# Tile 4 of the band heads turned through VectorE and DRAM, in two tours of two tiles per head, and the keys' second copy on VectorE

## The chip, the cores and the metric

The kernel runs on one core of a Trainium2 chip. A core has TensorE (PE in the profile) for matrix products, VectorE (DVE), ScalarE (ACT) and GpSimd (POOL) for elementwise work, and SyncE (SP), which here issues every DMA. The metric is the device time of one execution in microseconds: a median of three runs, with the lowest and the highest beside it.

## The reference

One layer of a streaming encoder, for a prompt of 1024 rows and a sample of 32 rows with the same weights (model width 1024). After a norm, one projection gives queries, keys, values and gates for two groups of eight heads of width 64. Group A is a band attention with a softmax and a relative-position bias; group B is a stick-breaking attention, strictly causal.

```
def band_attention(q, k, v, q_pos, k_pos, bias_table):      # group A
    s = jnp.einsum('bqhd,bkhd->bhqk', q, k).astype(jnp.float32) * ATTN_SCALE
    s = s + bias_table[:, rel].astype(jnp.float32)[None]
    s = jnp.where(ok[None, None], s, NEG_INF)               # own chunk of 64 and the 8 before it
    w = jax.nn.softmax(s, axis=-1).astype(v.dtype)
    return jnp.einsum('bhqk,bkhd->bqhd', w, v)

def stick_breaking(q, k, v, q_pos, k_pos):                  # group B
    z = jnp.einsum('bqhd,bkhd->bhqk', q, k).astype(jnp.float32) * ATTN_SCALE
    log_1m = jnp.where(causal, jax.nn.log_sigmoid(-z), 0.0)
    after = lax.cumsum(log_1m, axis=3, reverse=True) - log_1m
    w = jnp.where(causal, jnp.exp(jax.nn.log_sigmoid(z) + after), 0.0).astype(v.dtype)
    return jnp.einsum('bhqk,bkhd->bqhd', w, v)

y = jnp.concatenate([oa * silu(ga), ob * silu(gb)], axis=-1) @ w_out
h = h + rmsnorm(y, g_post)
h = h + sigmoid(h @ w_ple_gate) * (p @ w_ple)
```

Everything is fp32. The keys and values of both groups are outputs too.

## The kernel before

**Numbers in two parts.** An fp32 operand is held as a high part that TensorE takes in its faster fp32r format and a low part, the rest. A product is two or three fp32r products. In the names, `kd` is the high part of a head's keys, in both halves of the 128 partitions, `kl` the low part, `L` the queries (high part in one half, low in the other), `v2` the values, `wTh` and `wTl` the turned attention weights, high and low.

**Stages.** The program records all its operations in Python and then puts them in an order (`Recorder.order`, lines 485 to 559). There is a stage "first" (norm, turning of x, first projections), eight stages 0 to 7, and a stage "last" (output projection, norm, gate). Stages 0, 2, 4 and 6 hold the attention of two A heads each (pairs A0 to A3), stages 1, 3, 5 and 7 that of two B heads each. Woven between them stand the projections of the next pair (`mm_kB`, `mm_qB`, `mm_vB` and so on), which are what TensorE does while an attention tile waits for other engines. Stages 2, 3, 6 and 7 also hold the sample's attention.

**One A head** (`attention`, line 965). The 1024 queries are eight tiles of 128. Tile i reads `cost(i)` blocks of 128 keys: 1, 2, 3, 4 for the tiles 0 to 3, and 5 (640 keys) for the tiles 4 to 7. `scores` (line 997) does the products `SA<-kdA,LA` and `SA<-kl,LA`, VectorE adds the bias and takes the minimum, ScalarE does the exponentials into `be`. Then the weights have to be turned so that keys lie on the partitions. `weights_t` (line 1060) has two ways:

- With TensorE: per block a product `ptw<-ident,be` of 128x128 into PSUM; ScalarE rounds it into `wTh`, VectorE subtracts into `wTl`.
- Through DRAM, for the tiles in `TURNED`: VectorE turns 32x32 squares (`om<-be`), and when the last tile of a tour (`ROUNDS`) is there, SyncE writes the tour to DRAM (`swapA<-om`) and reads it back with four DMAs (`wTl<-swapA`), one for each 32 partitions. Then ScalarE rounds each tile (`wTh<-wTl`) and GpSimd subtracts (`wTl<-wTl,wTh`).

Before, the A tiles 5, 6 and 7 went through DRAM, in one tour of three tiles, and the tiles 4, 0, 1, 2, 3 through TensorE. When a set of four tiles is turned, `values` (line 1106) does `PVA<-wTh,v2A` and `PVA<-wTl,v2A`; set 1 of an A head is the tiles 4 to 7, set 0 the tiles 0 to 3. B heads have three tours of one tile each, and nothing of that changes.

**The keys.** `prep_k` (line 783) makes `kd` and `kl` of a head: a copy into the head's own half of the partitions and one into the other half, both by ScalarE, and the subtraction by GpSimd. `first_head` (line 799) does the same for the very first head in two pieces.

**The order.** `Recorder.order` plays the program with rough costs. On each engine the ready operation with the smallest key goes first; the key is the place in the recorded program plus a number of `AHEAD_OF`, by engine, kind of tile and stage. Every engine then runs its list strictly in that order, and SyncE issues all DMAs in one list; before it issues a DMA it also waits for the one eight places earlier to have ended (the `DMAHW` waits in its list).

All compute instructions are issued at line 572, so the profile is read by names of tiles.

Of the kernel before, what the change touches and what calls it, by code (L numbers as in the profile page):

```python
# [15 lines left out]
SEQ = 1024  # L16
# [10 lines left out]
NT = 9  # L27
STAGES = ("first", 0, 1, 2, 3, 4, 5, 6, 7, "last")
AHEAD_OF = {
    ("ACT", "Kh"): (0, 0, 0, 0, 430, 0, 0, 0, 200, 0),  # L30
    ("ACT", "L"): (0, 0, 46, 25, 452, 0, 112, 50, 0, 0),
    ("ACT", "Qfs"): (0, 0, 0, 0, 400, 0, 0, 0, 0, 0),
# [10 lines left out]
    ("ACT", "php"): (0, 0, 0, 0, 0, 0, 0, 0, 0, 175),  # L43
    ("ACT", "ple"): (0, 0, 0, 0, 0, 0, 0, 0, 0, 315),
    ("ACT", "stk"): (0, 0, 0, 0, 0, 96, -610, 0, 0, 0),
    ("ACT", "stq"): (0, 0, 0, 0, 0, -93, 0, 0, 0, 0),
    ("ACT", "stv"): (0, 0, -42, 0, 400, 0, 0, 0, 0, 0),
    ("ACT", "v"): (0, 0, 0, 0, 461, 0, 0, 0, 0, 0),
    ("ACT", "wTh"): (0, 93, 3, 89, 487, 0, 142, 52, -161, 0),
    ("ACT", "wh"): (0, 0, 405, 0, 0, 90, -480, -51, 364, 0),  # L50
    ("ACT", "whS"): (0, 0, 0, 0, 0, 0, 0, 0, 0, -93),
    ("ACT", "whs"): (0, 0, 0, 149, 0, 0, 0, 0, 0, 0),
    ("ACT", "x"): (0, 0, 0, 0, 0, 0, 0, 0, 0, -418),
    ("ACT", "xS"): (0, 0, 0, 0, 0, 0, 0, 0, 0, 25),
    ("DVE", "Kcs"): (0, 0, 0, 530, 0, 0, 0, 0, 100, 0),
    ("DVE", "Kl"): (0, 0, 0, 0, 0, 0, 0, 421, 0, 0),
    ("DVE", "L"): (0, 0, 0, 400, 0, 0, 0, 46, 0, 0),
    ("DVE", "Qls"): (0, 0, 0, 0, 0, 0, 0, 0, 54, 0),
# [3 lines left out]
    ("DVE", "diags"): (0, 0, 0, 400, 0, 0, 0, 0, 0, 0),  # L62
    ("DVE", "hnl"): (-100, 0, 0, 0, 0, 0, 0, 0, 0, 0),
# [4 lines left out]
    ("DVE", "sum"): (0, 0, 0, -109, 0, 0, 0, 0, 0, 0),  # L68
    ("DVE", "uu"): (0, 0, 0, 0, 0, 0, 0, 0, 0, -381),
    ("DVE", "vt"): (0, 165, 0, 0, -170, -75, 367, -88, 0, 0),  # L70
    ("DVE", "wTl"): (0, 0, 70, 0, 75, 50, 0, 100, -213, 0),
# [13 lines left out]
    ("POOL", "sgg"): (0, 0, 0, 0, 0, 0, 0, 0, 200, 0),  # L85
    ("POOL", "ug"): (0, 0, 0, 0, 0, 0, 0, 0, 0, -44),
    ("POOL", "wTl"): (0, 0, 0, 0, 400, 0, 465, 0, 0, 0),
# [15 lines left out]
}  # L103

TURNED = {"A": (5, 6, 7), "B": (4, 5, 6)}
ROUNDS = {"A": ((5, 6, 7),), "B": ((4,), (5,), (6,))}
GATES = ("A0", "A1", "A2", "A3", "B0", "B1", "B2", "B3")
SHARE = {7: 8}  # L110
SETS = {"A": ((0, 1, 2, 3), (4, 5, 6, 7)), "B": ((0, 1, 2, 3), (4, 5), (6, 7))}
TILES = {"A": (5, 6, 7, 4, 0, 1, 2, 3), "B": (6, 7, 5, 4, 0, 1, 2, 3)}
LAST = (7, 6, 5, 4, 3, 2, 1, 0)
LAG_G = 1
LAG_T = 2
# [10 lines left out]
def f(ap):  # L126

    return ap.bitcast(F32)
# [449 lines left out]
def stream_step(  # L578
# [7 lines left out]
    nc = rec  # L586
# [30 lines left out]
    hnl = [hnp.tile([P, KD, CH], F32R, tag=f"hnl{c}", name=f"hnl{c}") for c in range(NCH)]  # L617
# [15 lines left out]
    qsS = const.tile([P, 4, NS], F32, tag="qsS", name="qsS")  # L633
# [137 lines left out]
    KDh, KLD, Lq, V2 = {}, {}, {}, {}  # L771

    def halves(h):
        return slice(h * HD, (h + 1) * HD), slice((1 - h) * HD, (2 - h) * HD)

    def low_keys(h):

        if h not in KLD:
            KLD[h] = opnd[h].tile([P, SEQ], F32R, tag=f"kl{h}", name=f"kl{h}")
            nc.gpsimd.memset(f(KLD[h][halves(h)[1]]), 0.0)  # L780
        return KLD[h]

    def prep_k(nm, h, st):
        r, o = halves(h)
        kd = opnd[h].tile([P, SEQ], F32R, tag=f"kd{h}", name=f"kd{nm}{h}")
        kl = low_keys(h)
        nc.scalar.copy(kd[r], st[r, 0:SEQ])
        nc.scalar.copy(kd[o], st[r, 0:SEQ])
        nc.gpsimd.tensor_tensor(kl[r], st[r, 0:SEQ], f(kd[r]), ALU.subtract)
        KDh[h] = kd  # L790

# [7 lines left out]
    def first_head(k, st, cols):  # L799

        r, o = halves(0)
        if k == "q":
            if not cols.start:
                Lq[0] = opnd[0].tile([P, SEQ], F32R, tag="L0", name="LA00")
            nc.scalar.copy(Lq[0][r, cols], st[r, cols])
            nc.vector.tensor_tensor(Lq[0][o, cols], st[r, cols], f(Lq[0][r, cols]), ALU.subtract)
            return
        if not cols.start:
            KDh[0] = opnd[0].tile([P, SEQ], F32R, tag="kd0", name="kdA00")
            low_keys(0)  # L810
        nc.scalar.copy(KDh[0][r, cols], st[r, cols])
        nc.scalar.copy(KDh[0][o, cols], st[r, cols])
        nc.gpsimd.tensor_tensor(KLD[0][r, cols], st[r, cols], f(KDh[0][r, cols]), ALU.subtract)

    def prep_v(nm, h, tok):
# [149 lines left out]
    def attention(ab, p, h):  # L965
# [31 lines left out]
        def scores(i):  # L997
# [27 lines left out]
            else:  # L1025
# [7 lines left out]
                nc.scalar.activation(w1[:, 0:n], w0[:, 0:n], AF.Exp, bias=m[:, last:last + 1], scale=-1.0, accum_out=one[:, 8 * h + i:8 * h + i + 1])  # L1033
                if h and i == TILES["A"][-1]:
                    nc.vector.reciprocal(one, one)
# [24 lines left out]
        def weights_t(i):  # L1060
# [5 lines left out]
            hi, lo = (spot(g, x, i) for x in wT[g])  # L1066
            if i in TURNED[ab]:
                tour = next(x for x in ROUNDS[ab] if i in x)
                own, _, _, group, _ = laid(g)
# [329 lines left out]
    for n in range(-1, 8):  # L1399
        a = len(order)  # L1400
        if n < 7:
            ab, p = pairs[n + 1]
# [158 lines left out]
    ple = Ple(True)  # L1561
# [75 lines left out]
    L, R = HALF  # L1637
# [17 lines left out]
    ple = Ple(False)  # L1655
# [422 lines left out]
```

## Time and profile before

| | before |
|---|---|
| median of 3 runs (lowest to highest) | 774.18 us (773.89 to 775.28) |
| the profiled execution: time, and its span | 773.29 us, 771.5 us |
| granted TensorE clock, mean | 0.999 |
| instructions in the trace | 14229 |
| DMA moved, mean rate | 165.35 MB, 214 GB/s |

The profiled execution's time is 1.79 us more than its span (what lies around the span), and 0.89 us less than the median of the runs. The prediction shows the lines of the views as it comes to them. "Busy" is the time in which an engine had an instruction under way; a wait row names the engine that waited, for what, the sum in us, how often, and the longest.

### The profile page before, as it was taken

The numbers are of one execution on the slowest core, as the hardware profiler recorded it, in microseconds if no ns is written. First come the engines' busy times: TensorE is split into PE (matmuls) and PEld (weight loads), VectorE is DVE, ScalarE is ACT, GpSimd is POOL, SyncE is SP. The second block draws the span as 40 slices with busy tenths as digits, with TensorE's granted clock in tenths as the row PEclk, the third lists the DMA queues.
The fourth block names the chain that finished last, engine by engine and source line by source line (L and its number), as shares of the span: only waits on it lengthen the run. The fifth ranks groups of instructions, "written<-read, shape, count | busy, mean of one in ns | idle before, by whom it ended". The sixth has DMA issues, their size and how long they took to land.

```text
span 771.5 us, 14229 instructions
## 1 busy us (share of the span) xinstructions
PE 757.7 (98%) x4502; PEld 703.8 (91%) x4502; DVE 577.2 (75%) x1029; ACT 543.3 (70%) x1139; POOL 507.3 (66%) x547
## 2 busy tenths in 40 slices
PE   8999999999999999899999999999999999999997
PEld 6999999999999999899999899999998877888786
DVE  6727567687688778768797578789455787898975
ACT  6557887788688768798896687555338878766461
POOL 5734778985638657569994737778552639797533
PEclk9999999999999999999999999999999999999999
DMA  8637977759776557975759888869679867759644
GB/s 294 234 116 198 251 197 228 213 145 280 160 186 191 135 153 237 248 194 172 208 173 251 191 226 203 252 179 268 174 252 309 287 206 230 261 182 384 222 146 137
DMA packets 198398, 165.35 MB, mean 214 GB/s; under 512 B 65890, under 2 KB 165386, under 8 KB 198323
## 3 DMA queue, kind: packets, MB, share of 16 engines
q1 hardware_dynamic: 198322, 164.44, 73.4%
q8 instruction: 36, 0.59, 0.3%
q14 instruction: 40, 0.32, 0.2%
HBM read 105.72 MB, written 58.91 MB: 213 GB/s over the span
## 4 chain that ended last, share of the span: by engine, by line
PE 86%; DMA 5%; SPq 3%; ACT 2%; DVE 2%; issue 1%; POOL 1%; DVEq 0%; POOLq 0%; ACTq 0%
PE mm_qA L572 6%; PE mm_kA L572 6%; PE mm_vA L572 6%; PE mm_gB L572 6%; PE mm_kB L572 6%; PE mm_vB L572 4%; PE PVB L572 4%; PE SB L572 4%; SPq L572 3%; PE mm_qB L572 3%; PE SA L572 3%; PE mm_gA L572 3%; PE PVA L572 3%; PE ple L572 3%; PE g1P L572 3%; PE o3P L572 3%
## 5 line engine op out<-in xcount | busy, mean ns | idle before, releaser
L572 POOL TENSOR_TENSOR be<-be,om 128x1024 f32<-128x1024 f32 (+8 forms) x66 | 81.5, 1242 | 47.0 <-DVE om L572 20.7
L572 DVE TENSOR_TENSOR_SCAN om<-om,SB 128x384 f32<-128x384 f32 (+5 forms) x96 | 91.5, 964 | 17.9 <-ACT om L572 10.6
L572 POOL TENSOR_TENSOR wTl<-wTl,wTh 128x640 fp32r<-128x640 f32 (+2 forms) x42 | 72.7, 1749 | 15.3 <-ACT wTh L572 9.5
L572 ACT ACTIVATE be<-SB 128x512 f32<-128x512 f32 (+5 forms) x96 | 45.7, 496 | 11.9 <-PE SB L572 8.2
L572 ACT ACTIVATE om<-SB 128x384 f32<-128x384 f32 (+5 forms) x96 | 44.4, 494 | 13.6 <-DVE SB L572 8.4
L572 ACT ACTIVATE be<-be,statA 128x640 f32<-128x640 f32 (+3 forms) x64 | 44.4, 695 | 9.4 <-DVE statA L572 9.2
L572 DVE STREAM_TRANSPOSE om<-be 128x640 f32<-128x640 f32 (+2 forms) x48 | 42.9, 899 | 2.4 <-POOL be L572 1.1
L572 ACT CAST wTh<-wTl 128x640 fp32r<-128x640 f32 (+2 forms) x48 | 35.9, 778 | 10.5 <-DMA wTl<-swapA 7.1
L572 POOL TENSOR_TENSOR oB<-oB,oB 128x256 f32<-128x256 f32 x32 | 26.5, 848 | 14.6 <-DMA oB<-in_w_out_dram 14.6
L572 POOL TENSOR_TENSOR kl<-stkB,kdB 64x1024 fp32r<-64x1024 f32 x8 | 19.7, 2461 | 20.4 <-ACT kdB L572 20.3
L572 DVE CUSTOM_DVE_ANT_0 be<-SA,biasA 128x320 f32<-128x320 f32 (+3 forms) x64 | 30.1, 480 | 3.6 <-PE SA L572 2.8
L572 PE MATMUL SB<-kl,LB 128*128 128x384 f32 (+5 forms) x96 | 32.5, 345 | 0.0
L572 PE MATMUL SB<-kdB,LB 128*128 128x384 f32 (+5 forms) x96 | 32.4, 342 | 0.0
L572 ACT CAST wTh<-ptwB 128x512 fp32r<-128x512 f32 (+3 forms) x48 | 22.8, 481 | 11.8 <-PE ptwB L572 10.1
L572 DVE TENSOR_TENSOR wTl<-ptwB,wTh 128x512 fp32r<-128x512 f32 (+3 forms) x48 | 25.9, 546 | 6.0 <-ACT wTh L572 5.2
L572 PE MATMUL SA<-kl,LA 128*128 128x320 f32 (+2 forms) x96 | 30.1, 316 | 0.0
L572 PE MATMUL SA<-kdA,LA 128*128 128x320 f32 (+2 forms) x96 | 29.9, 313 | 0.0
L572 DVE TENSOR_TENSOR SB<-SB,maskb 128x128 f32<-128x128 f32 x64 | 18.0, 293 | 15.5 <-PE SB L572 14.4
L572 DVE TENSOR_TENSOR wTl<-ptwA,wTh 128x512 fp32r<-128x512 f32 (+3 forms) x48 | 22.5, 480 | 8.1 <-ACT wTh L572 5.3
L572 POOL TENSOR_TENSOR gB<-gB,gB 128x256 f32<-128x256 f32 x32 | 24.0, 771 | 1.5 <-DMA gB<-in_w_ple_gate_dram 1.4
L572 PE MATMUL PVB<-wTl,v2B 128*128 128x256 f32 (+1 forms) x144 | 24.8, 294 | 0.0
L572 POOL TENSOR_TENSOR h<-h,x 128x512 f32<-128x512 f32 (+1 forms) x18 | 23.8, 1345 | 0.2 <-DVE h L572 0.2
(700 smaller groups left out, 2669.3 us busy)
## 6 DMA issues: line engine op xcount, KB each, us to landing
swapA<-om SPq DMA_DIRECT2D x8, 960.0 KB, 6.9
wTl<-swapA SPq DMA_DIRECT2D x32, 240.0 KB, 5.1
oB<-in_w_out_dram SPq DMA_DIRECT2D x16, 256.0 KB, 3.5
sum_dro<-oB SPq DMA_DIRECT2D x16, 256.0 KB, 3.6
gB<-in_w_ple_gate_dram SPq DMA_DIRECT2D x16, 256.0 KB, 4.4
sum_drg<-gB SPq DMA_DIRECT2D x16, 256.0 KB, 2.7
x<-in_x_prompt_dram SPq DMA_DIRECT2D x16, 256.0 KB, 3.9
h_dr<-h SPq DMA_DIRECT2D x8, 512.0 KB, 3.6
```

What stands on the lines that cost most here:

```text
L572: getattr(getattr(tc.nc, o.what[0]), o.what[1])(*args, **kw)
```

## The change

The tile sets and the order of tiles of group A:

```
-TURNED = {"A": (5, 6, 7), "B": (4, 5, 6)}
-ROUNDS = {"A": ((5, 6, 7),), "B": ((4,), (5,), (6,))}
+TURNED = {"A": (4, 5, 6, 7), "B": (4, 5, 6)}
+ROUNDS = {"A": ((4, 5), (6, 7)), "B": ((4,), (5,), (6,))}
-TILES = {"A": (5, 6, 7, 4, 0, 1, 2, 3), "B": (6, 7, 5, 4, 0, 1, 2, 3)}
+TILES = {"A": (4, 5, 6, 7, 0, 1, 2, 3), "B": (6, 7, 5, 4, 0, 1, 2, 3)}
```

The keys' second copy, in `prep_k` and in `first_head`:

```
         nc.scalar.copy(kd[r], st[r, 0:SEQ])
-        nc.scalar.copy(kd[o], st[r, 0:SEQ])
+        nc.vector.tensor_copy(kd[o], st[r, 0:SEQ])
...
         nc.scalar.copy(KDh[0][r, cols], st[r, cols])
-        nc.scalar.copy(KDh[0][o, cols], st[r, cols])
+        nc.vector.tensor_copy(KDh[0][o, cols], st[r, cols])
```

And the numbers of `AHEAD_OF`, nearly all of them, for instance:

```
-    ("SP", "swap"): (0, 415, -50, 0, 0, 0, 0, 0, 0, 0),
+    ("SP", "swap"): (0, 0, 0, 0, 0, 0, 0, 0, -200, 0),
```

What the new numbers do is seen in the order of the instructions. Three places follow.

**TensorE, stage 4, head A20** (the first head of pair A2; `A20_4` is its tile 4). Before, behind the scores of its tiles, the tile's transposes stand between products of the projection `mm_qB2` and scores of the next head A21:

```order
L572 MATMUL ptwB11_3_0_4108<-ident_160,be_193 128x128 x4
L572 MATMUL mm_qB2_1_4049<-hnh1_155,wh_qB2_0_3774 128x352
L572 MATMUL ptwA20_4_0_4117<-ident_160,be_193 128x128 x4
L572 MATMUL mm_qB2_1_4049<-hnh1_155,wh_qB2_0_3774 128x352 x2
L572 MATMUL mm_qB2_1_4049<-hnh1_155,wh_qB2_1_3785 128x352 x4
L572 MATMUL SA21_5_0_4142<-kdA21_3865,LA21_3869 128x320
L572 MATMUL PVB11_0_4135<-wTh_655,v2B11_3230 128x512
```

Now, at the same place of TensorE's list, behind the scores of head A20's last tile:

```order
L568 MATMUL SA20_3_0_4118<-kdA20_3279,LA20_3284 128x512
L568 MATMUL SA20_3_0_4118<-kl0_664,LA20_3284 128x512
L568 MATMUL SA21_4_0_4126<-kdA21_3858,LA21_3863 128x320
L568 MATMUL SA21_4_0_4126<-kl1_709,LA21_3863 128x320
L568 MATMUL mm_qB2_1_4025<-hnh1_163,wh_qB2_0_3752 128x352
L568 MATMUL mm_qB2_1_4025<-hnh1_163,wh_qB2_1_3761 128x352
L568 MATMUL PVB11_0_4097<-wTh_733,v2B11_3196 128x512
L568 MATMUL PVB11_0_4097<-wTh_733,v2B11_3196 128x384
L568 MATMUL PVB11_0_4097<-wTh_733,v2B11_3196 128x256
L568 MATMUL PVB11_0_4097<-wTh_733,v2B11_3196 128x128
L568 MATMUL ptwA20_0_0_4114<-ident_168,be_201 128x128
```

The `ptwA20_4` products are gone (a row of four and, some rows later, one of one), and the next head begins with its tile 4 instead of its tile 5.

**SyncE's list of DMAs, the same head.** Before, from the write of its one tour to the four reads (`out_4_dram<-ktB2` are outputs of keys, `gB` and `sum_drg` loads and stores of weight sums for the last stage, `o_dr` an attention result):

```order
L572 DMA swapA20_7_133<-om_179 128x1920
L572 DMA wr_qA3_0_4066<-in_w_in_dram 128x4x128
L572 DMA out_4_dram<-ktB2_3935 32x32x32
L572 DMA out_3_dram<-vtA2_3509 128x4x128
L572 DMA out_4_dram<-ktB2_3935 32x32x32 x3
L572 DMA ks_drB_91<-ktB2_3935 128x32
L572 DMA wr_qA3_1_4122<-in_w_in_dram 128x4x128
L572 DMA o_dr5_68<-otB11_1_0_3772 64x256
L572 DMA sum_drg_86<-gB220_3960 128x512
L572 DMA biasA30_4152<-r_dr_87 128x640
L572 DMA sum_drg_86<-gB120_3959 128x512
L572 DMA wTl_170<-swapA20_7_133 32x12x160 x4
```

Now, from some rows behind the first tour's write (`swapA20_5`) to the last read of the second:

```order
L568 DMA wr_qA3_1_4088<-in_w_in_dram 128x4x128
L568 DMA sum_drg_86<-gB120_3956 128x512
L568 DMA swapA20_7_138<-om_187 128x1280
L568 DMA sum_drg_86<-gB110_3958 128x512
L568 DMA biasA30_4167<-r_dr_87 128x640
L568 DMA wTl_178<-swapA20_5_137 32x8x160 x4
L568 DMA o_dr5_68<-otB11_0_0_3790 64x256
L568 DMA o_dr5_68<-otB11_0_1_3989 64x256
L568 DMA gB210_4222<-in_w_ple_gate_dram 128x512
L568 DMA wTl_178<-swapA20_7_138 32x8x160 x4
```

Where one write and four reads stood there are now two writes and eight reads, each of two tiles; the second tour's reads stand behind those of the first, and the key outputs that stood between write and reads have moved ahead of the second tour's write.

**ScalarE and VectorE, stage 3, the keys of head A20.** Before, both copies stand on ScalarE, with operations of the B head before (`SB10`) between them:

```order
L572 CAST kdA20_3295<-stkA2_3044 64x1024
L572 ACTIVATE om_179<-SB10_1_0_3253 128x256
L572 ACTIVATE be_193<-SB10_1_0_3253 128x256
L572 ACTIVATE om_179<-SB10_2_0_3254 128x384
L572 CAST kdA20_3295<-stkA2_3044 64x1024
```

Now one stands on ScalarE in that place, and the other on VectorE, between the sample's keys (`Kl0sB0`, and a transpose of the cached ones) and the low weights of head B10:

```order
L568 TENSOR_TENSOR Kl0sB0_3034<-be_201,Kh0sB0_3014 128x512
L568 CAST kdA20_3279<-stkA2_2936 64x1024
L568 STREAM_TRANSPOSE be_201<-be_201 128x512
L568 TENSOR_TENSOR wTl_178<-ptwB10_0_0_3193,wTh_733 128x128
```

Counted over the whole program, TensorE's list has 4462 products instead of 4502 (40 of `ptwA` fewer), SyncE's 40 DMAs more.

More of the change, by code (lines that the diff above doesn't have):

```diff
@@ L29 @@
 AHEAD_OF = {
-    ("ACT", "Kh"): (0, 0, 0, 0, 430, 0, 0, 0, 200, 0),
-    ("ACT", "L"): (0, 0, 46, 25, 452, 0, 112, 50, 0, 0),
-    ("ACT", "Qfs"): (0, 0, 0, 0, 400, 0, 0, 0, 0, 0),
[10 rows of a table removed]
[L43 to L57, printed above, removed]
@@ L58 @@
-    ("DVE", "Qls"): (0, 0, 0, 0, 0, 0, 0, 0, 54, 0),
[3 rows of a table removed]
-    ("DVE", "diags"): (0, 0, 0, 400, 0, 0, 0, 0, 0, 0),
-    ("DVE", "hnl"): (-100, 0, 0, 0, 0, 0, 0, 0, 0, 0),
[4 rows of a table removed]
[L68 to L71, printed above, removed]
[13 rows of a table removed]
-    ("POOL", "sgg"): (0, 0, 0, 0, 0, 0, 0, 0, 200, 0),
-    ("POOL", "ug"): (0, 0, 0, 0, 0, 0, 0, 0, 0, -44),
@@ L87 @@
-    ("POOL", "wTl"): (0, 0, 0, 0, 400, 0, 465, 0, 0, 0),
[15 rows of a table removed]
-}
-TURNED = {"A": (5, 6, 7), "B": (4, 5, 6)}
-ROUNDS = {"A": ((5, 6, 7),), "B": ((4,), (5,), (6,))}
+    ("ACT", ""): (0, 0, 0, 0, 0, 0, 0, 0, 0, 19),
+    ("ACT", "Kh"): (0, 0, 0, -265, 0, 0, 0, 0, -225, 0),
+    ("ACT", "L"): (0, 0, 0, 0, 401, 0, 200, 0, 0, 0),
+    ("ACT", "Qfs"): (0, 0, 0, 0, 398, 0, 0, 0, 0, 0),
[4 rows of a table added]
+    ("ACT", "junk"): (0, 0, 0, 0, 0, 0, 0, 0, 0, 401),
[5 rows of a table added]
+    ("ACT", "stk"): (0, 0, 0, 0, -25, 0, -120, 0, 0, 0),
+    ("ACT", "stq"): (0, 0, 0, 0, 0, 0, 167, -580, 0, 0),
@@ new lines @@
+    ("ACT", "stv"): (0, -140, 93, 0, 436, -102, 0, 0, 0, 0),
+    ("ACT", "wTh"): (0, 0, 0, 50, 400, 0, 298, 77, 0, 0),
[4 rows of a table added]
+    ("DVE", "Kcs"): (0, 0, 0, 0, 0, 0, 0, 88, 0, 0),
[4 rows of a table added]
+    ("DVE", "diags"): (0, 0, 0, 121, 0, 0, 0, 0, 0, 0),
+    ("DVE", "hnl"): (-495, 0, 0, 0, 0, 0, 0, 0, 0, 0),
[7 rows of a table added]
+    ("DVE", "wTl"): (0, -408, 441, 70, 124, 89, -87, 453, 94, 0),
[8 rows of a table added]
+    ("POOL", "Qfs"): (0, 0, 0, 0, 0, 0, 0, 0, -41, 0),
+    ("POOL", "be"): (0, 0, 203, 0, 0, 0, 359, 0, -200, 0),
+    ("POOL", "kl"): (0, 0, 0, 0, -550, 0, 0, 0, 0, 0),
@@ L109 @@
+    ("POOL", "ogg"): (0, 0, 0, 0, 0, 0, 0, 0, 86, 0),
+    ("POOL", "om"): (0, 0, 0, 0, 0, 0, -356, 0, -28, 0),
+    ("POOL", "qsS"): (0, 0, 0, 0, 0, 200, 0, 0, 0, 0),
[18 rows of a table added]
+}
+TURNED = {"A": (4, 5, 6, 7), "B": (4, 5, 6)}
+ROUNDS = {"A": ((4, 5), (6, 7)), "B": ((4,), (5,), (6,))}
 GATES = ("A0", "A1", "A2", "A3", "B0", "B1", "B2", "B3")
```

89 rows, old and new, of the table AHEAD_OF are left out of this document.

## The prediction

> **What bounds the kernel now.** First the page's busy times. TensorE (PE) is busy for nearly the whole span:
>
> ```profile
> span 771.5 us, 14229 instructions
> PE 757.7 (98%) x4502; PEld 703.8 (91%) x4502; DVE 577.2 (75%) x1029; ACT 543.3 (70%) x1139; POOL 507.3 (66%) x547
> ```
>
> Busy does not yet mean paced by itself, so next the chain of work that ended last. It shows long runs of products at one pace, and at one place something else:
>
> ```profile
> 59.91 3.80 PE mm_vA L572 x24
> 72.63 0.55 PE ptwA L572 x5
> 318.34 7.57 DMA wTl<-swapA
> 325.94 1.99 ACT wTh L572 x3
> 327.97 1.79 PE PVA L572 x10
> ```
>
> 24 products of 352 columns take 3.80 us, 0.16 us each, with nothing between: there TensorE's own work sets the time. The three rows from 318.34 on are the exception: a read of a tour, then its roundings, then the product that waited. What TensorE waits for, summed:
>
> ```profile
> PE PVA L572 <- ACT wTh L572: 2.3, 2, 2.0
> PE ptwA L572 <- DVE wlsA L572: 1.8, 2, 0.9
> PE idle L572 <- DVE newh L572: 1.3, 1, 1.3
> PE ptx L572 <- DVE be L572: 1.3, 1, 1.3
> PE PVsB L572 <- DVE Vl2sB L572: 0.8, 1, 0.8
> PE PVA L572 <- DVE v2A L572: 0.6, 1, 0.6
> PE ptwB L572 <- POOL be L572: 0.3, 1, 0.3
> ```
>
> `idle` and `ptx` are the start. The attention holds 2.3 + 1.8 + 0.8 + 0.6 + 0.3 = 5.8 us of waits, and these plus products are all that a change of the attention can gain. By stage (us, then busy us of each engine, clock, DMA share, GB/s), for A0, A2, A3 and the last B pair:
>
> ```profile
> 62.00:118.00 56.00, 56.00 (x360) 54.88 (x359) 39.18 (x90) 44.70 (x95) 35.91 (x44) 1.00 0.80 219
> 288.00:348.00 60.00, 57.96 (x381) 56.35 (x380) 46.70 (x104) 50.88 (x106) 39.78 (x37) 1.00 0.81 220
> 400.00:470.00 70.00, 68.20 (x442) 66.32 (x441) 50.12 (x109) 51.41 (x112) 40.58 (x43) 1.00 0.86 219
> 470.00:582.00 112.00, 110.88 (x718) 109.08 (x717) 80.95 (x130) 58.61 (x132) 77.90 (x84) 1.00 0.76 219
> ```
>
> TensorE idles 2.0 us in A2 and 1.8 us in A3, the A stages with the waits for `wTh`; no other engine is busy for more than 85% of an A stage, but the DMA engines are at 0.80 to 0.86.
>
> **The change part by part.** *TensorE.* Tile 4 has five blocks, so five transposes go in each of eight heads: 40. The row of five above takes 0.55 us, 0.11 us each: 40 x 0.109 = **4.4 us** less. They stand in a row of products without gaps, so all of it is on the path. Nothing is added on TensorE.
>
> *ScalarE and VectorE around the tile.* The rows, busy us in all and mean ns of one:
>
> ```profile
> L572 ACT CAST wTh<-ptwA 128x512 fp32r<-128x512 f32 x16 | 9.3, 579 | 2.0 <-PE ptwA L572 1.9
> L572 ACT CAST wTh<-ptwA 128x128 fp32r<-128x128 f32 x16 | 4.1, 275 | 1.2 <-PE ptwA L572 1.0
> L572 ACT CAST wTh<-wTl 128x640 fp32r<-128x640 f32 x32 | 21.7, 724 | 9.6 <-DMA wTl<-swapA 7.1 <-DMA be<-in_cache_a_v_dram 2.3
> L572 DVE TENSOR_TENSOR wTl<-ptwA,wTh 128x512 fp32r<-128x512 f32 x16 | 10.9, 684 | 2.5 <-ACT wTh L572 1.9 <-PE PVA L572 0.6
> L572 DVE TENSOR_TENSOR wTl<-ptwA,wTh 128x128 fp32r<-128x128 f32 x16 | 4.1, 284 | 4.3 <-ACT wTh L572 2.2 <-ACT om L572 2.0
> L572 DVE STREAM_TRANSPOSE om<-be 128x640 f32<-128x640 f32 x32 | 26.4, 832 | 1.1 <-ACT be L572 1.0
> L572 POOL TENSOR_TENSOR wTl<-wTl,wTh 128x640 fp32r<-128x640 f32 x30 | 48.7, 1645 | 9.5 <-ACT wTh L572 7.6 <-DMA oggA<-o_dr 1.6
> ```
>
> ScalarE trades 8 x (0.58 + 0.28) for 8 x 0.72, VectorE 8 x (0.68 + 0.28) for 8 x 0.83: about 1 us less on each. GpSimd takes over 8 x 1.65 = 13.2 us, 3.3 us per A stage, where it is busy for 36 of 56 us; a stage has room, so I cost it at nothing, and without that cover it is at most the 13.2.
>
> *The keys' copy.* Sixteen heads, 1.05 us each on ScalarE (half of the 14 + 16 below; the first head's two pieces taken as one more):
>
> ```profile
> L572 ACT CAST kdA<-stkA 64x1024 fp32r<-64x1024 f32 x14 | 14.7, 1048 | 4.5 <-PE SB L572 4.3
> L572 ACT CAST kdB<-stkB 64x1024 fp32r<-64x1024 f32 x16 | 16.8, 1051 | 0.3
> L572 DVE CAST wTl<-grow 1x1024 fp32r<-1x1024 f32 x1 | 0.7, 682 | 0.1
> L572 DVE CAST Vh0sB<-be 128x512 fp32r<-128x512 f32 x2 | 0.8, 405 | 0.0
> L572 DVE CAST Vh0sA<-be 128x512 fp32r<-128x512 f32 x2 | 2.5, 1232 | 3.1 <-DMA be<-in_cache_a_v_dram 3.1
> ```
>
> ScalarE loses 16.8 us. VectorE has no such copy of 64x1024 before; the nearest is 0.68 us for 1024 columns, and the bounds are those 0.68 and, from the two 512-column rows, 0.83 us more (1.23 against 0.41). I take 0.68: 11 us more on VectorE, in stages where it is busy for 75%. TensorE needs the copy only for a head's first scores, far ahead of which both queues place it: nothing on the path, 13 us (16 x 0.83) at the other end. ScalarE's gain is nothing on the path either, since no wait row of TensorE names a late copy; it may shorten the waits that end at `wTh`.
>
> The 405 and 1232 ns are one operation of one shape; here the Trainium skill has a rule that speaks against the edit: "SBUF — State Buffer", Who interferes with whom, says that a copy or cast on VectorE can take a port pair that it shares with GpSimd, and that whichever of the two starts second is blocked until the other ends. The trace agrees in that the cast's time varies threefold; that the port did it, no row shows. By the rule a copy beside the GpSimd subtraction of the same keys could stand still for all of it; what the sum would be by it is worked out from rows at the last rival below.
>
> *The tours.* 16 writes of 640 KB in place of 8 of 960, and 64 reads of 160 KB in place of 32 of 240 (each with its median us to landing, and below SyncE's time to issue):
>
> ```profile
> swapA<-om SPq DMA_DIRECT2D x8, 960.0 KB, 6.9
> wTl<-swapA SPq DMA_DIRECT2D x32, 240.0 KB, 5.1
> swapB<-om SPq DMA_DIRECT2D x8, 448.0 KB, 2.8
> wTl<-swapB SPq DMA_DIRECT2D x32, 112.0 KB, 2.9
> L572 SPq DMA_DIRECT2D wTl<-swapA x32: 563/616/736, 80.1 to 458.1; - x32
> ```
>
> Between the two sizes by bytes (37.5% of the way), a 640 KB write is 2.8 + 1.5 = 4.3 us, a 160 KB read 3.7: a round trip of 8.0 us, not 12.0. And behind the last landing stand two roundings and two subtractions instead of three (0.72 and 1.65 us less). Against it: the tour that ends last now waits for the fourth tile, not the third, and its reads stand in SyncE's list behind the four of the first tour, 4 x 0.62 = 2.5 us. So the last weights of set 1 come between 4 us earlier and, if every DMA keeps the large one's time, some 3 us later (2.5 and a tile's 0.83 turning). In the order the products that fill the time between tile 7's scores and `PVA` are about as many as before. I take **0** for the waits, with both ends kept: -2.9 us (both `PVA` rows go) and, at 3 us in the two heads that wait now, +6.
>
> *DMA.* 8 x 2 x 0.32 = 5.1 MB more: at the 219 GB/s of an A stage 5.8 us of transfers per A stage, beside the products. *The order anew* has no row: the waits for `wlsA`, `PVsB` and `ptwB` (2.9 us) can go or others come; 0.
>
> **Sum:** 773.29 - 4.4 + 0 = 768.9 for the profiled execution; the median is 0.9 above that, so **769.8 us**. A measurement of this kernel can tell about 0.2%, 1.5 us, from no change.
>
> **The rivals.** *The waits go too.* Shorter round trips and a freer ScalarE take the 2.9 us of `PVA` waits as well: 766.9, and 764.0 if all 5.8 went. For it: the largest wait stands behind three roundings in a row. Against it: it came from DMAs that landed late.
>
> *Given back at `PVA`.* The second tour begins a tile later. If `PVA` then waits 0.55 us more in each head, the 4.4 are gone; two more waits like the 2.0 of the list make 773.8. For it: two `PVA` rows already wait. Against: the smaller tours.
>
> *The DMA engines become the bound, and it is slower.* In A3, five stretches of 5 us:
>
> ```profile
> 415.00:420.00 5.00, 5.00 (x35) 4.98 (x34) 3.39 (x10) 3.39 (x11) 0.61 (x3) 1.00 1.00 312
> 420.00:425.00 5.00, 5.00 (x36) 5.00 (x35) 2.75 (x7) 3.25 (x5) 2.49 (x2) 1.00 1.16 200
> 425.00:430.00 5.00, 5.00 (x34) 4.97 (x33) 1.99 (x4) 2.62 (x7) 4.29 (x6) 1.00 1.12 247
> 430.00:435.00 5.00, 4.40 (x27) 4.01 (x26) 3.53 (x3) 3.60 (x7) 4.57 (x5) 1.00 0.89 177
> 435.00:440.00 5.00, 4.07 (x28) 3.70 (x27) 2.25 (x5) 2.08 (x5) 4.27 (x6) 1.00 0.67 154
> ```
>
> The DMA share is 1 or more for 15 us, and right behind it TensorE idles 1.5 us. If a transfer added there delays TensorE by its whole time, A2 and A3 lose 5.8 us each: 769.8 + 11.6 = 781.4. It ends slower once added waits pass 4.4 + 1.5 = 5.9 us, half of that price. Against it: A0 has a share of 0.80 and no wait at all.
>
> *The copies are held by GpSimd.* At the upper bound of 0.83 us in each of 16 heads it is 13 us of VectorE, and with half of that reaching a head's first scores 6.6: 776.4. Against it: those scores wait nowhere now. (This is where the Trainium skill's rule of "SBUF — State Buffer", Who interferes with whom, would lead.)
>
> **How the numbers follow.** Forecast 0.48 (its own range 768.0 to 771.6, from waits that come or go by 1.8 us); the waits go too 0.20; given back 0.16; DMA bound 0.11; copies held 0.05. Faster is the first two, 0.68; same 0.16; slower 0.16. The range runs from 765.5, most of the second case, to 776.0, which takes in the waits' upper end (769.8 + 6) and leaves out most of the last two.
>
> **What would show it.** Right: `ptwA` x80 and PE busy near 753; `PVA` waits of 3 us or less in all; kd casts on VectorE near 0.7 us; shorter landings of `swapA` and `wTl`. Wrong: a `PVA` wait in several heads (given back); TensorE idle behind stretches with a DMA share over 1 (DMA bound); kd casts of 1.5 us or more and waits of `SA` or `SB` products (copies held). The forecast falls if new waits anywhere, the first stage included, exceed 2 us.

## The result, and the profile after

| | time (lowest to highest) | ratio to before, 95% interval |
|---|---|---|
| before, 4 runs beside it | 774.03 us (772.6 to 775.28) | |
| changed, 4 runs | 783.74 us (781.56 to 785.63) | 1.0125 [1.0092, 1.0159] |
| the prediction | 769.8 us (765.5 to 776.0) | 0.994 |

The change costs 9.7 us; the prediction had it gain 4.4. The profiled execution took 781.56 us, span 779.8. The page of the changed kernel, busy times and the tours' DMAs:

```profile
span 779.8 us, 14229 instructions
PE 757.0 (97%) x4462; PEld 698.9 (90%) x4462; DVE 592.3 (76%) x1038; ACT 525.2 (67%) x1114; POOL 529.9 (68%) x555
swapA<-om SPq DMA_DIRECT2D x16, 640.0 KB, 3.9
wTl<-swapA SPq DMA_DIRECT2D x64, 160.0 KB, 4.3
```

TensorE has its 40 products fewer, ScalarE is 18 us less busy, the smaller tours do land sooner each (6.9 and 5.1 before). All that the change was to remove is removed. But TensorE's busy time fell by 0.7 us only (757.7 before), and the span is 8.3 us longer: TensorE idles 22.8 us in place of 13.8. Its list of waits in the changed kernel (sum in us, how often, longest):

```profile
PE PVA L568 <- ACT wTh L568: 4.1, 3, 2.3
PE PVB L568 <- ACT wTh L568: 3.9, 3, 1.6
PE PVB L568 <- DVE v2B L568: 2.9, 1, 2.9
PE ptwsA L568 <- POOL be L568: 1.3, 2, 1.0
PE ptwA L568 <- DVE wTl L568: 0.9, 1, 0.9
```

The waits before were 5.8 us in the attention; here the five rows alone are 13.1. Two kinds are new or larger: products of weights and values that wait for a rounding `wTh`, in A stages and now in B stages too, and one single wait of 2.9 us for `v2B`, which no row of before has. The three `PVB` waits for a rounding stand in stage 7, the last B pair, where no tour of group A runs; the longest of them, and the two longest of `PVA` (in A1 and A2):

```profile
505.05 0.93 PE L568 MATMUL PVB<-wTh,v2B 128*128 128x256 f32 x6 [1.62 <-ACT wTh L568]
207.64 1.50 PE L568 MATMUL PVA<-wTh,v2A 128*128 128x512 f32 x8 [1.37 <-ACT wTh L568]
334.46 1.50 PE L568 MATMUL PVA<-wTh,v2A 128*128 128x512 f32 x8 [2.31 <-ACT wTh L568]
```

Two places were followed back.

**The wait for `v2B`.** Stage 1, the values of head B00; VectorE's rows (start, us), then GpSimd's, of the changed kernel:

```profile
136.37 1.80 DVE L568 CAST kdA<-stkA 64x1024 fp32r<-64x1024 f32 x1
138.20 4.61 DVE L568 TENSOR_TENSOR v2B<-vtB,v2B 128x512 fp32r<-128x512 f32 x1
...
135.14 2.41 POOL L568 TENSOR_TENSOR kl<-stkA,kdA 64x1024 fp32r<-64x1024 f32 x1
...
137.59 1.17 POOL L568 TENSOR_TENSOR oB<-oB,oB 128x256 f32<-128x256 f32 x1
138.72 1.82 POOL L568 TENSOR_TENSOR wTl<-wTl,wTh 128x768 fp32r<-128x768 f32 x1
140.50 1.76 POOL L568 TENSOR_TENSOR be<-be,om 128x896 f32<-128x896 f32 x1
```

The new copy begins while GpSimd subtracts the low part of the same keys (`kl`, until 137.55) and ends 0.62 us behind that: 1.80 us for an operation that takes 0.69 alone. The subtraction `v2B` behind it then begins among three GpSimd operations without a gap, and ends at 142.81, 0.55 us behind the last of them (142.26): 4.61 us for one whose median is 0.93.

**A wait for `wTh`.** Stage 4, head A20, SyncE's reads of the two tours and ScalarE's roundings, of the changed kernel; then the same product `PVA` in the kernel before:

```profile
320.75 2.57 SPq L568 DMA_DIRECT2D wTl<-swapA  x4
326.11 2.98 SPq L568 DMA_DIRECT2D wTl<-swapA  x4
329.32 1.36 ACT L568 CAST wTh<-wTl 128x640 fp32r<-128x640 f32 x2 [4.67 <-DMA wTl<-swapA]
333.06 1.34 ACT L568 CAST wTh<-wTl 128x640 fp32r<-128x640 f32 x2
...
327.97 1.50 PE L572 MATMUL PVA<-wTh,v2A 128*128 128x512 f32 x8 [2.04 <-ACT wTh L572]
```

The first tour's reads are all issued by 323.32, but its rounding begins at 329.32, six microseconds later, and ScalarE stands 4.67 us at the head of its list for them. What is queued behind is late by that: 2.6 us of other work and then the second tour's rounding, for which `PVA` waits. But the second tour is late too: its last read, issued at 328.54, landed 4.3 us later, only some 0.2 us before its rounding begins. And the wait is not new: the kernel before waited 2.04 us at the same product. The 1.8 us that `PVA` waits more in all are mostly 0.42 us in A0 and the 1.37 us in A1, which it did not have.

So there were three theories. **W:** the new numbers of the order brought the waits. **D:** the turning's 5.1 MB and 40 DMAs land the weights late. **K:** a copy on VectorE is held beside GpSimd and holds what is behind it.

### The profile page after: what moved, and what is told of

Its sections match the earlier page's. It is cut to its first block, busy times and chain, and to the rows that moved or that the text cites. A ratio compares the mean times of both kernels' runs of the same rounds, so it can differ in the third digit from the quotient of the medians.

```text
span 779.8 us, 14229 instructions
## 1 busy us (share of the span) xinstructions
PE 757.0 (97%) x4462; PEld 698.9 (90%) x4462; DVE 592.3 (76%) x1038; ACT 525.2 (67%) x1114; POOL 529.9 (68%) x555
## 2 busy tenths in 40 slices
DMA packets 204156, 170.58 MB, mean 219 GB/s; under 512 B 66529, under 2 KB 170121, under 8 KB 204082
## 4 chain that ended last, share of the span: by engine, by line
PE 59%; DMA 8%; SPq 4%; ACT 4%; DVE 3%; issue 2%; POOL 1%; ACTq 0%; POOLq 0%; DVEq 0%
PE mm_gB L568 5%; PE mm_vA L568 4%; DMA wTl<-swapA 4%; SPq L568 4%; PE PVB L568 4%; PE mm_qA L568 4%; PE mm_kB L568 3%; PE o3P L568 3%; PE g1P L568 3%; PE o1P L568 3%; PE o2P L568 2%; PE o0P L568 2%; PE g0P L568 2%; PE g2P L568 2%; PE g3P L568 2%; PE SB L568 2%
## 5 line engine op out<-in xcount | busy, mean ns | idle before, releaser
L568 POOL TENSOR_TENSOR be<-be,om 128x1024 f32<-128x1024 f32 (+8 forms) x66 | 85.5, 1301 | 25.2 <-DVE om L568 18.5
L568 POOL TENSOR_TENSOR wTl<-wTl,wTh 128x640 fp32r<-128x640 f32 (+2 forms) x50 | 85.7, 1731 | 21.7 <-ACT wTh L568 10.1
L568 ACT CAST wTh<-wTl 128x640 fp32r<-128x640 f32 (+2 forms) x56 | 41.8, 773 | 30.4 <-DMA wTl<-swapA 13.1
L568 ACT ACTIVATE om<-SB 128x384 f32<-128x384 f32 (+5 forms) x96 | 44.8, 493 | 20.5 <-DVE SB L568 14.6
L568 ACT ACTIVATE be<-be,statA 128x640 f32<-128x640 f32 (+2 forms) x64 | 44.3, 693 | 13.8 <-DVE statA L568 13.6
L568 DVE STREAM_TRANSPOSE om<-be 128x640 f32<-128x640 f32 (+2 forms) x56 | 49.5, 890 | 2.3 <-POOL be L568 1.1
L568 ACT ACTIVATE be<-SB 128x384 f32<-128x384 f32 (+5 forms) x96 | 45.0, 496 | 9.2 <-PE SB L568 5.2
L568 DVE CUSTOM_DVE_ANT_0 be<-SA,biasA 128x320 f32<-128x320 f32 (+2 forms) x64 | 30.0, 480 | 4.2 <-POOL biasA L568 2.1
L568 POOL TENSOR_TENSOR oB<-oB,oB 128x256 f32<-128x256 f32 x32 | 25.8, 826 | 10.2 <-DMA oB<-in_w_out_dram 10.1
L568 PE MATMUL PVB<-wTh,v2B 128*128 128x256 f32 (+1 forms) x144 | 22.2, 286 | 6.8 <-ACT wTh L568 3.9
L568 PEld LDWEIGHTS PVB<-wTh,v2B 128*128 128x128 f32 x144 | 20.7, 188 | 8.2 <-ACT wTh L568 4.7
```

The source lines that it names most:

```text
L568: getattr(getattr(tc.nc, o.what[0]), o.what[1])(*args, **kw)
```

## The experiments

### Single edits, ordered anew

Eight kernels combine the three parts of the change: the turning, the copies, and the numbers of the order (old, new or none).

```
-TURNED = {"A": (5, 6, 7), "B": (4, 5, 6)}
+TURNED = {"A": (4, 5, 6, 7), "B": (4, 5, 6)}
...
-        nc.scalar.copy(kd[o], st[r, 0:SEQ])
+        nc.vector.tensor_copy(kd[o], st[r, 0:SEQ])
...
-    ("SP", "swap"): (0, 415, -50, 0, 0, 0, 0, 0, 0, 0),
+    ("SP", "swap"): (0, 0, 0, 0, 0, 0, 0, 0, -200, 0),
```

Turning alone: 

> The kernel before with tile 4 turned through DRAM in two tours per head; copies on ScalarE and the old numbers of the order. Theory W (the new order brings the waits): the 4.4 us of transposes are gained, so about 770 us, with a few us of misfit of the old numbers: 768 to 774. Theory D (the turning itself, its tours, 40 more DMAs and 5.1 MB, lands the weights late): 780 or more, with waits for wTh behind the DMA of swapA or swapB of 5 us more than before. Theory K (the copies on VectorE, held by GpSimd): about 770.

Copies alone: 

> The kernel before with only the keys' second copy on VectorE, old numbers. Theory K: 778 to 784, kdA on VectorE 1.3 us in the mean and single VectorE subtractions of 3 us or more beside GpSimd work. Theory W and theory D: 774, at most 1.5 us either way.

New numbers alone: 

> The kernel before with only the new numbers of the order. Theory W: 780 or more, waits at PVA, PVB and ptwA. But numbers fitted to another program can also misfit here, so a slow time speaks only weakly for W; a time of 776 or less speaks against it. Theories D and K: 774 to 777.

Turning and copies: 

> The turning and the copies of the change, with the old numbers of the order. Theory W: 768 to 775, faster than the changed kernel's 783.7 by more than 8. Theory D: 780 or more. Theory K: 778 or more. If the old numbers misfit badly, 785 or more, which would speak against W: the new numbers then repair something.

Turning and new numbers: 

> The changed kernel with the keys' second copy back on ScalarE (new numbers, new turning). Theory K (copies on VectorE held by GpSimd): 775 or less, no VectorE subtraction v2B of 4 us and no PVB wait behind it. Theories W and D: 782 to 786; the 16.8 us back on ScalarE may add a few us at wTh.

Copies and new numbers: 

> The changed kernel with the old turning (tiles 5, 6, 7 in one tour, tile 4 on TensorE), copies on VectorE, new numbers. Theory D: 776 or less, since the tours are the old ones. Theory W: 784 or more, with 4.4 us more of TensorE's transposes on top. Theory K: 784 to 788.

Before without numbers: 

> The kernel before with an empty table: the order follows the recorded program alone. A neutral base: 780 to 810 us.

Changed without numbers: 

> The changed kernel with an empty table. Beside the kernel before with an empty table it shows what turning and copies do without any fitted numbers. Theory W: 3 to 6 us faster than that. Theory D or K: 5 us or more slower than that.

| turning | copies | numbers | us | ratio to before |
|---|---|---|---|---|
| - | - | none | 803.55 | 1.0365 [1.0308, 1.0422] |
| yes | yes | none | 800.97 | 1.0334 [1.0288, 1.0381] |
| yes | - | old | 805.48 | 1.0408 [1.0374, 1.0443] |
| - | yes | old | 795.68 | 1.0278 [1.0238, 1.0318] |
| yes | yes | old | 799.58 | 1.0315 [1.0263, 1.0367] |
| - | - | new | 798.46 | 1.0307 [1.0272, 1.0341] |
| yes | - | new | 800.26 | 1.0328 [1.0280, 1.0375] |
| - | yes | new | 790.91 | 1.0197 [1.0147, 1.0248] |

For turning alone theories W and K missed by 30 us and more, for copies alone K by 12 and the others by 20. The open bounds (D's "780 or more", W's) include what came, but a time 20 us beyond a bound speaks for no theory. One reason explains the misses: the numbers fit one program. They are worth 29.5 us to the kernel before (803.55 against 774.0) and 17.2 to the changed one (800.97 against 783.7). A program that differs by one part stands at 791 to 805 us, near the 801 to 804 without any numbers. No cause can be read from such a pair. The one pair that is fair, both without numbers, differs by 2.6 us: the intervals of the ratios overlap, the four times of each do not (802.4 to 804.0 and 800.2 to 801.0). The changed program is ahead there, near the 3 to 6 us of theory W and against the 5 us of loss that D and K gave. So whatever the bytes and the copies cost, they cost it in the fitted order, not in every order.

### Single edits in the changed kernel's own order

So the order was kept. An operation is recorded as before, and thus keeps its place in every engine's list; afterwards the engine that issues it, or the size of a DMA, is changed. The first three concern the copies (the first piece is for the changed kernel, for all copies or for head A10 alone; the second is for the kernel before):

```
         nc.vector.tensor_copy(kd[o], st[r, 0:SEQ])
+        rec.ops[-1].what = ("scalar", "copy")
...
         nc.scalar.copy(kd[o], st[r, 0:SEQ])
+        rec.ops[-1].what = ("vector", "tensor_copy")
```

All back to ScalarE: 

> The changed kernel with its own order kept to the last instruction; only the 17 second copies of the keys are issued by ScalarE, at the same places of the program. Theory K (a copy held by GpSimd holds VectorE): the 2.9 us wait PVB for v2B goes, 779 to 781 us, v2B on VectorE at 1.4 us or less each. Rival, the copies cost nothing on VectorE and ScalarE's 17 us more delay its roundings: 784 to 788, more waits for wTh.

Measured 780.09 us, 1.0084 [1.0051, 1.0116], the time that theory K gave. The wait for `v2B` is gone. `PVA` waits 5.0 us in place of 4.1, but `PVB` 2.3 in place of 3.9, so the rival's waits for `wTh` did not grow in sum. The interval overlaps that of the change.

Only head A10's: 

> The changed kernel in its own order; one second copy alone, that of head A10's keys (the cast of 1.8 us directly ahead of the 4.6 us subtraction v2B), is issued by ScalarE. Theory K: v2B starts before GpSimd's three operations in a row, takes 0.7 us, and the wait at PVB of 2.9 us goes: 780 to 781.5. Rival, v2B is held by the same three operations whatever stands ahead of it: 783 to 785 and v2B again over 3 us.

Measured **778.02 us, 1.0059 [1.0027, 1.0091]**: 5.1 us less than the change by the ratios. Both intervals together make such a difference uncertain by some 3.6 us. VectorE's and GpSimd's rows at that place:

```profile
135.41 1.55 DVE L568 TENSOR_TENSOR v2B<-vtB,v2B 128x512 fp32r<-128x512 f32 x1 [0.21 <-ACT v2B L568]
...
134.00 2.41 POOL L568 TENSOR_TENSOR kl<-stkA,kdA 64x1024 fp32r<-64x1024 f32 x1
```

`v2B` now begins beside `kl` and ends at 136.96, again 0.55 us behind the end of a GpSimd operation (136.41). It is held by one, not by three in a row, and nothing waits for it. TensorE's list is the same in both kernels, so its starts can be compared, ahead of the wait and behind it; first in the changed kernel, then with the one copy back:

```profile
139.28 0.80 PE L568 MATMUL mm_qA<-hnh,wl_qA 128*128 128x352 f32 x4
142.96 0.59 PE L568 MATMUL PVB<-wTh,v2B 128*128 128x256 f32 x3 [2.88 <-DVE v2B L568]
...
138.14 0.81 PE L568 MATMUL mm_qA<-hnh,wl_qA 128*128 128x352 f32 x4
138.78 0.52 PE L568 MATMUL PVB<-wTh,v2B 128*128 128x256 f32 x3
```

The lead is 1.14 us ahead of this place and 4.18 us behind it: 3.0 us are gained here. The profiled executions differ by 4.8 us in span; that the rest comes from the copy is not shown. Theory K holds, with two corrections: the subtraction took 1.55 us, not 0.7, and the time came out below the 780 us and more that it gave.

The copies in the order of before: 

> The kernel before with its own order kept; only the 17 second copies are issued by VectorE at the same places. Prediction's step (copies hidden): 773 to 775.5. Theory K: 777 or more, with waits at SA, SB, PVB or a VectorE operation of 3 us or more.

Measured 785.95 us, 1.016 [1.0124, 1.0195], as theory K asked (777 or more) and well above it. The largest new wait names VectorE, and single copies are longer than any in the changed kernel:

```profile
PE SA L572 <- DVE statA L572: 3.1, 2, 1.6
L572 DVE CAST kdA<-stkA x9: 520/1547/3635, 42.6 to 405.9; 64x1024 fp32r<-64x1024 f32 x7, 64x704 fp32r<-64x704 f32 x1, 64x320 fp32r<-64x320 f32 x1
```

Next the bytes. The first tour of each A head carries its second tile only, so tile 4's weights are stale (the four reads are cut in the same way):

```
                 dma(dr, box["room"][:, 0:m * n * P])
+                less = ab == "A" and i == 5
+                if less:
+                    rec.ops[-1].args = (dr[:, n * P:], box["room"][:, n * P:m * n * P])
```

Tile 4 not moved: 

> The changed kernel in its own order with the same list of DMAs, but the first tour of each A head carries only its second tile (tile 4's weights are neither written to DRAM nor read back, so the output is not the reference's): the bytes are those of before, 165.3 MB. Theory D (the 5.1 MB added load the DMA engines and land the weights late): waits for wTh fall by 4 us or more, 779 or less. If the order alone sets when the weights land: 782 to 785.

Measured **773.42 us, 0.9995 [0.9964, 1.0027]**: 10.1 us less than the change by the ratios, for 5.25 MB (165.33 MB in its page, 170.58 in that of the change). SyncE's list has as many DMAs as in the changed kernel, so their number is not what is taken away. Head A20 again, the reads, the roundings, the product:

```profile
315.33 2.62 SPq L568 DMA_DIRECT2D wTl<-swapA  x4
320.70 0.71 ACT L568 CAST wTh<-wTl 128x640 fp32r<-128x640 f32 x1
321.94 0.73 ACT L568 CAST wTh<-wTl 128x640 fp32r<-128x640 f32 x1 [0.53 <-DMA wTl<-swapA]
328.20 1.50 PE L568 MATMUL PVA<-wTh,v2A 128*128 128x512 f32 x8 [0.16 <-ACT wTh L568]
```

(Tile 4's rounding waits for no read here; the second row is tile 5's.) From the last read's issue (317.95) to that row's start it is 4.0 us, not 6.0, ScalarE stands 0.53 us, and `PVA` waits 0.16 us instead of 2.31. The reads also begin earlier against TensorE's work: TensorE comes to `PVA` (its start less its wait) 12.7 us after the first read begins, in the changed kernel 11.4. Over the whole run `PVA` waits 0.5 us for `wTh` instead of 4.1. The stretches from the reads on, in the changed kernel and in this one (after PE to POOL: clock, DMA share, GB/s):

```profile
324.00:328.00 4.00, 4.00 (x27) 3.91 (x26) 3.74 (x14) 0.65 (x2) 0.29 (x2) 1.00 1.08 251
328.00:332.00 4.00, 4.00 (x25) 3.58 (x23) 1.22 (x3) 2.65 (x4) 1.82 (x2) 1.00 1.12 254
...
316.00:320.00 4.00, 4.00 (x28) 3.98 (x27) 3.81 (x10) 2.13 (x7) 0.00 (x0) 1.00 0.93 267
320.00:324.00 4.00, 4.00 (x27) 3.93 (x26) 3.74 (x14) 3.44 (x6) 2.74 (x4) 1.00 0.74 195
```

Theory D holds in its main point: without these bytes the weights are there in time. Two things limit it. The edit takes away more than the change brought: tile 4's rounding waits for no read at all, and the wait at this product, which the kernel before has too, is gone, so the 10.1 us (uncertain by 3.6) are not the price of the added bytes alone. And a share above 1 is a loose sign of late reads. In the run with one copy back the first tour's reads again took 6.0 us and ScalarE stood 4.50 us for them, with these shares:

```profile
316.00:320.00 4.00, 4.00 (x28) 4.00 (x28) 3.74 (x12) 1.21 (x3) 0.04 (x1) 1.00 1.00 213
320.00:324.00 4.00, 4.00 (x26) 3.91 (x25) 2.61 (x10) 1.32 (x3) 0.71 (x3) 1.00 0.94 230
```

Both edits: 

> The changed kernel in its own order with both edits: head A10's second copy on ScalarE and tile 4's weights not moved through DRAM (the output is not the reference's). If the held copy and the added bytes are two separate costs that make up the whole miss: 767 to 770, the prediction's sum. If they overlap (one wait behind the other): 772 to 775.

Measured **769.45 us, 0.9936 [0.9911, 0.9962]**. That is 14.6 us less than the change, where the two singly gave 5.1 + 10.1 = 15.2, and clear of the 772 to 775 expected if one hid behind the other: two separate costs. Its busy times and waits:

```profile
PE 756.0 (98%) x4462; PEld 700.8 (91%) x4462; DVE 592.6 (77%) x1037; ACT 527.2 (69%) x1115; POOL 529.4 (69%) x555
PE PVA L568 <- ACT wTh L568: 1.5, 2, 1.2
PE PVB L568 <- ACT wTh L568: 1.3, 2, 0.7
PE SB L568 <- DVE om L568: 1.1, 2, 1.0
```

The new numbers of the order are all in this kernel, and it is faster than before. So theory W is not needed for the loss as a whole. It has a part, though: the `PVB` waits of stage 7 are in every run with the whole of the changed kernel's order (1.3 to 3.9 us) and in none with that of before.

Other bytes taken away, the tours whole; of each output of keys a sixteenth of the rows or less is written:

```
                 dma(rows[:, :, q], x[q, 0:n]...)
+                rec.ops[-1].args = (rows[:, 0:2, q], x[q, 0:64]...)
```

> The changed kernel in its own order, tours whole; the writes of the keys' outputs carry a sixteenth or less of their rows (that output is incomplete), 3 MB less in packets of 128 bytes, most of it in the same stages as the tours. If it is the load of the DMA engines that lands the weights late: 779 or less, fewer waits for wTh. If it is the length of the tours themselves: 782 to 785.

Measured 778.83 us, 1.0066 [1.0043, 1.0090], with 167.69 MB in its page: 4.6 us less for 2.9 MB, 1.6 us per MB, where tile 4's bytes gave 10.1 for 5.25, 1.9 per MB. `PVA` waits 1.5 us in place of 4.1, `PVB` 3.5 in place of 3.9. So the load of the DMA engines costs time whoever makes it; each difference is uncertain by 3 us and more, too much to say that the two prices are one. Head A20 shows how it helped; the reads of the first tour, their rounding, the product, and two stretches:

```profile
317.05 4.01 SPq L568 DMA_DIRECT2D wTl<-swapA  x4
326.40 1.36 ACT L568 CAST wTh<-wTl 128x640 fp32r<-128x640 f32 x2 [1.32 <-DMA wTl<-swapA]
332.23 1.51 PE L568 MATMUL PVA<-wTh,v2A 128*128 128x512 f32 x8
320.00:324.00 4.00, 4.00 (x28) 3.98 (x27) 3.81 (x8) 2.30 (x6) 0.29 (x2) 1.00 1.07 197
324.00:328.00 4.00, 4.00 (x28) 4.00 (x27) 3.88 (x14) 2.52 (x5) 0.73 (x1) 1.00 1.14 193
```

The share is above 1 here too, and from the last issue (321.06) to the rounding it is still 5.3 us. But the reads begin 15.2 us before TensorE comes to `PVA`, in place of 11.4, and `PVA` waits for nothing. Here fewer bytes had the reads issued earlier, more than they had them land sooner.

### Three attempts to gain, and the form of the copy

Two kernels join early stages of the changed kernel (with the one copy back) to late stages of before, each half in its own order:

```
+NEW = (0, 1, 2)          # or (0, 1): pairs of A turned the new way
+def way(ab, p):
+    return "a" if ab == "A" and p not in NEW else ab
```

> Pairs A0 to A2 as in the changed kernel with the one copy on ScalarE, in its own order; pair A3, and everything from stage 6 on, as in the kernel before, in the order of before. Head A30 began 4.1 us earlier than before in the run with one copy back, and from there to the end that run lost 7.6 us. If the loss sits in the late stages: 769 to 771.5, faster than both kernels. If the early gain was only other work put off: 774 or more.

> The same with pairs A0 and A1 turned the new way and everything from stage 4 on as before. Head A20 began 4.4 us earlier than before in that run: 769 to 772 if the gain is kept, 774 or more if it was work put off.

Measured 785.58 us, 1.0168 [1.0127, 1.0209], and 781.85 us, 1.0096 [1.0072, 1.0120]. The early lead of 4 us is lost in both. But behind the seam stand new waits (`PVA` 3.4 us at 471.36 in the first, 4.3 us at 335.12 in the second), so these say nothing on where the change pays, nor whether the lead was work put off.

The copy in another form (`tensor_scalar` times 1.0, in place of `tensor_copy`): 

> The changed kernel in its own order; the 17 second copies are made by VectorE as products with 1.0 (another form of instruction, same operands, same places). If a hold belongs to the form of the copy: all sixteen of 64x1024 of one length (0.7 or 1.2 us), none of 1.8; the time is 777 to 781 if v2B at head B0 then starts before GpSimd's three operations, 782 to 784 if the longer product makes it start beside them and it is held itself. If GpSimd holds any VectorE work: products up to 1.8 us or more, 783 to 786.

Measured 782.35 us, 1.0112 [1.0082, 1.0141], like the change. The products' lengths (shortest/median/longest ns, then first and last start):

```profile
L568 DVE TENSOR_SCALAR kdB<-stkB x8: 689/690/1786, 88.0 to 454.8; 64x1024 fp32r<-64x1024 f32 x8
136.84 4.62 DVE L568 TENSOR_TENSOR v2B<-vtB,v2B 128x512 fp32r<-128x512 f32 x1
```

0.69 alone and 1.79 held, as the copies, and `v2B` is held again. Another form of the same work does not escape; whether every operation of VectorE would be held isn't answered.

The keys' outputs issued later, no byte less (some 8 us added to their place in SyncE's list, on top of the one copy back): 

> one_copy_back (778.0) with the writes of the keys' outputs issued some 8 us later in SyncE's list, so that fewer of them stand among the tours; no byte less. If when the bytes meet decides: 773 to 776, fewer waits for wTh at PVA. If their amount decides: 777 to 780.

Measured 782.35 us, 1.0105 [1.0074, 1.0135]. That is above both expectations. It has a new wait of 4.8 us at an `SA` product of stage 0 (at 73.07), behind VectorE, which stood 5.5 us for a late `out_dram<-ktA`; `PVA` still waits 3.5 us. Moving these bytes by one step for all stages only moved the collision, so whether a better time for them exists stays open. No version here that computes the whole reference beats the kernel before.

## Why the prediction was wrong

- **TensorE, 4.4 us less, "all of it on the path": shown only in part.** `ptwA` counts 80, but the prediction's own sign, busy near 753, did not come: 757.0 us, and 756.0 with the two costs taken out. Where the other 3 us and more went, no run here shows. With the two costs out the kernel takes 769.45 us where the sum said 769.8; but there TensorE is 1.7 us less busy and idles 1.6 us less (12.2 against 13.8), so this agreement is in part luck.
- **Tours, "a round trip of 8.0 us": right in size.** 3.9 + 4.3 = 8.2 us as medians. But a median says nothing of the reads that TensorE waits for; head A20's took 6.0 us from the last issue to the rounding (6.9 in the kernel before).
- **"I take 0 for the waits": the first step that failed.** TensorE's listed waits in the attention went from 5.8 to 14.5 us. The term looked at `PVA` in two heads, which waits 1.8 us more, inside the bounds of -2.9 and +6. It left out the other products: the 2.9 us for `v2B`, the 3.9 us of `PVB`, and 1.3 us at the sample's `ptwsA`.
- **DMA, "5.8 us of transfers per A stage, beside the products": the same error as a term.** Taking tile 4's bytes away gave 10.1 us, near the 11.6 at which the rival "the DMA engines become the bound" was priced. It got a chance of 0.11 because A0 has no wait; after the change A0 waits 0.42 us and A1 1.37. The mechanism is not the rival's, a transfer's whole time added, and the price fits it by luck: the weights are issued and land later in several stages. The 1.5 us idle that the prediction cited behind its stretches of A3 were two waits for VectorE (`v2A` 0.6, `wlsA` 0.9), not for a DMA.
- **The keys' copy, "nothing on the path": the second step that failed.** The mean was 1.29 us for `kdA` and 1.00 for `kdB`, inside the bounds of 0.68 and 1.51, and no first score waited. The cost came from what stood behind one copy on VectorE: 3.0 us at that place, 5.1 by the medians, where the rival said 6.6 by another way. The Trainium skill's rule that the prediction weighed ("SBUF — State Buffer", Who interferes with whom) said that the second starter is blocked until the first ends; the trace agrees, and in this one place goes further, since `v2B` was blocked over three GpSimd operations.
- **ScalarE and GpSimd around the tile, 0: not seen in any wait row** of the changed kernel that names GpSimd's `wTl`.
- **"The order anew, 0": near it, as a net figure.** The waits for `wlsA` and `PVsB` (2.6 us) are gone, and the new order has `PVB` waits of 1.3 to 3.9 us. But an order can hide or show such costs, and 17 to 30 us hang on it; a 0 without bounds was too bold. Both costs are shown in this one order alone; without any numbers the change gains 2.6 us.
- **The chances.** The two rivals were treated as if only one could come, and each was thought unlikely. Both came: 774.0 - 4.4 + 10.1 + 5.1 = 784.8, against 783.7 measured; with such wide terms this fits better than it could be expected to.

## What to carry to other kernels

A mean DMA share below 1 does not show that a transfer is hidden: compare when the waited-for reads are issued and land with when TensorE comes to their product, and look at every strict list that a late read can block, not only at the last reader. A copy moved to an idle engine is priced by what stands behind it there and by what GpSimd does at that moment. To find what an edit costs in a kernel whose order is fitted, keep the order to the last instruction and change one operation in place; ordering anew changes more than the edit.

## What the runs showed of the hardware

- **VectorE beside GpSimd: held by one operation in most places, once by three.** `v2B` took 4.61 us for a subtraction of two operands in SBUF (0.65 at its shortest before), ended 0.55 us behind the third of them, and 4.62 in the run with products. This is no rule: in the same kernel a like subtraction came in at the first boundary, between two GpSimd operations without a gap.

```profile
305.53 1.27 DVE L568 TENSOR_TENSOR v2A<-vtA,v2A 128x512 fp32r<-128x512 f32 x1
304.40 1.85 POOL L568 TENSOR_TENSOR wTl<-wTl,wTh 128x768 fp32r<-128x768 f32 x1
306.22 1.74 POOL L568 TENSOR_TENSOR wl_vB<-wr_vB,wh_vB 128x512 fp32r<-128x512 f32 x1
```

It ended at 306.80, 0.55 us behind the first. Why `v2B` missed two such boundaries stays open. GpSimd is held as well: `oB`, right behind the copy, took 1.17 us where two of them take 1.44 in the run with one copy back.
- **An idle TensorE loses its clock.** In the changed kernel without numbers TensorE waits 6.2 us at 480.8; the stretch in it and two behind it (span, TensorE's busy us, weight loads, VectorE, ScalarE, GpSimd, then clock):

```profile
481.00:484.00 3.00, 0.00 (x0) 0.00 (x0) 1.44 (x2) 2.04 (x4) 1.81 (x2) 1.00 0.85 198
488.00:492.00 4.00, 4.00 (x17) 4.00 (x16) 1.33 (x5) 2.31 (x7) 4.00 (x3) 0.50 0.86 214
492.00:496.00 4.00, 4.00 (x29) 3.88 (x27) 2.86 (x5) 1.67 (x5) 2.42 (x3) 0.98 0.50 99
```

The clock is 0.50 from the first product behind the wait (486.9) until 492, and 17 products run in 4 us where 29 do later: an estimate from these rows is 2.5 us lost beyond the wait itself. Shorter waits did it too, but not each time. The same 2.88 us wait for `v2B`, in the changed kernel and in the run with short key outputs, has behind it:

```profile
143.00:146.50 3.50, 3.50 (x26) 3.50 (x27) 3.20 (x5) 3.34 (x8) 0.79 (x1) 1.00 0.31 104
143.00:146.50 3.50, 3.50 (x17) 3.50 (x17) 2.89 (x4) 2.47 (x7) 1.34 (x1) 0.51 0.02 5
```

In the second 17 products run where 26 do in the first: some 1.7 us more, for one wait. In the run with one copy back the 2.31 us wait at `PVA` (327.85) is followed by a mean of 0.59 from 328 to 332, in the changed kernel's profile it is not. The changed kernel's other executions fit this: 781.56 us (the profiled one) and 782.91 have mean clocks of 0.998 and 0.996, 784.57 and 785.63 have 0.990 and 0.991. So part of what a wait costs in the medians is the clock behind it; how much, the profiles of single executions do not show.
